# Forming the sample queries of the cross-attention in the stream of sample keys, and starting the output projection with head 3's rows

## The chip, the core and the metric

The kernel runs on one core of a Trainium2 chip. The metric is the device time of one execution in microseconds (us). TensorE (PE) multiplies matrices into PSUM; VectorE (DVE), ScalarE (ACT) and GpSimd (POOL) do the rest; SyncE (SP), ACT and POOL issue the transfers (DMA). Each engine takes its instructions in one fixed order, which was settled when the program was built, and waits at an instruction until what it needs is there.

## The reference, cut to what matters

The reference is one layer of a decoder for 1024 prompt tokens and 8 sample sequences of 4 tokens (32 tokens). The part that the change touches is the cross-attention of 4 heads of 256 channels to 256 memory tokens. The prompt attends to a memory computed in the kernel, each sample sequence to its own cached keys and values:

```python
    xn = rms_norm(x, p['ln2_g'])
    cq = rms_norm((xn @ p['ca_wq']).reshape(bsz, t, CA_HEADS, CA_HEAD_DIM), p['ca_q_norm_g'])
    s = jnp.einsum('bqhd,bmhd->bhqm', cq, mem_k.astype(cq.dtype)).astype(f32) * (CA_HEAD_DIM ** -0.5)
    pr = jax.nn.softmax(s, axis=-1).astype(x.dtype)
    co = jnp.einsum('bhqm,bmhd->bqhd', pr, mem_v.astype(x.dtype)).reshape(bsz, t, D_MODEL)
    x = x + co @ p['ca_wo']
```

## The kernel before

Every float32 product is made of three passes (`mm3`: high x high, high x low, low x high), each operand being split into a high and a low part. The 1056 columns (1024 prompt and 32 sample tokens) are worked on in three blocks, `TB`: block 0 and 1 of 384 columns, block 2 of 256 prompt and 32 sample columns.

The cross-attention runs three streams that a small planner (`par`) interleaves by weights, and a scheduler then fixes the order on each engine:

- `wq_head(h)` projects the queries of head h, blocks in the order 2, 0, 1 (PE matmuls `pp<-Xh,whi` and so on, 24 for each half head and block), and leaves the squares for their norms (`pq`), from which `query_scale` makes the scales `crs`.
- `ca_head(h)` is the prompt's attention: scores `S` (6 matmuls a tile of 128 queries), softmax on DVE and ACT, transposes of the probabilities (`pts`), products with the values (`po`). In block 2 it calls `sample_query(h)`, which scales the 32 sample queries (`pb` on PE, four products into `Qc` on DVE).
- `sample_keys(h)` waits for that, then loads the cached keys of the 8 sequences (`kt`, 256 KB each, two buffers, issued by SP), transposes each one (four PE matmuls `pt<-ident,kt`, copied to `KT` by ACT) and, after four of them, adds their scores to `Ssm`. Call these sets 1 to 8 of a head.

After head 3 comes `sample_softmax` and then the output projection `ca_wo`, with two streams: `wo_stage`, whose `part(d, b)` sums 8 row chunks of 128 (k = 0 to 7) for output chunk d and block b, and `sample_values`, which loads 16 value tiles (`vt`, 512 KB, three buffers, issued by POOL) and multiplies them (`Op`). Chunks 0 to 5 (heads 0 to 2) went to DRAM (`coT`) and are loaded again as `ms` and split to `Mh`, `Ml`; chunks 6 and 7 (head 3) stay on chip as `coh`, `col`. Block 2 of the projection waits for the end of `sample_values`.

Of the kernel before, what the change touches and what calls it, by code (L numbers as in the profile page):

```python
# [69 lines left out]
def hymba_step(ctx: ExitStack, tc: tile.TileContext, A: dict, O: dict, upto=99, dbg=None):  # L70
# [1560 lines left out]
    with ExitStack() as p5:  # L1631
# [7 lines left out]
        Qc = ca.tile([128, 2, NB, 32], F32, name="Qc", bufs=1)  # L1639
        Ssm = ps_q.tile([128, NMEM], F32, name="Ssm")  # L1640
        hq = {}
        queries = set()
        scaled, late = set(), []
        BORD = [2, 0, 1]
        CKB = 1
# [5 lines left out]
        def wq_head(h):  # L1651
            while h >= 2 and blocks[h - 2] < 3:
                yield None
            kr = ca.tile([128, 2, NMEM], F32, tag="kr", name="kr", bufs=1)
            vr = ca.tile([128, 2, 256], F32, tag="kr", name="vr", bufs=1)
            kh = ca.tile([128, 2, NMEM], F32R, tag="ckh", name="ckh")
            kl = ca.tile([128, 2, NMEM], F32R, tag="ckl", name="ckl")
            vh = ca.tile([128, 2, 256], F32R, tag="cvh", name="cvh")
            vl = ca.tile([128, 2, 256], F32R, tag="cvl", name="cvl")
            w = [load_cols(A['ca_wq'][0], 2 * h + z, GT[:, 16:24]) for z in range(2)]  # L1660
            nc.sync.dma_start(out=kr, in_=mkT_d[256 * h:256 * h + 256, :].rearrange("(k p) m -> p k m", p=128))
            split(kh, kl, kr)
            nc.sync.dma_start(out=vr, in_=mv_d[:, 256 * h:256 * h + 256].rearrange("(c p) d -> p c d", p=128))
            split(vh, vl, vr)
            cqt = {}
            ssq = ca.tile([128, 9], F32, tag="ssq", name="ssq")
            nc.vector.memset(ssq, 1.0)
            rs = ca.tile([128, 9], F32, tag="crs", name="crs")
            hq[h] = (kh, kl, vh, vl, cqt, rs)
            for oi, bi in enumerate(BORD):  # L1670
                t0, n = TB[bi]
                while h >= 1 and blocks[h - 1] < oi:
                    yield None
                ch = ca.tile([128, 2, 384], F32R, tag="ch", name="ch", bufs=4)
                cl = ca.tile([128, 2, 384], F32R, tag="cl", name="cl", bufs=4)
                sqs = []
                for z in range(2):
                    pp = ps_j.tile([128, 384], F32, tag="pj", name="pp")
                    for k in range(KD):
                        mm3(pp[:, :n], w[z][0][:, k], w[z][1][:, k], Xh[:, k, t0:t0 + n], Xl[:, k, t0:t0 + n],  # L1680
                            k == 0, k == KD - 1)
                        if k % 2:
                            yield 6 * n / 2.4
                    if late:
                        late.pop()()
                        yield 350
                    split_g(ch[:, z, :n], cl[:, z, :n], pp[:, :n], GT[:, 124 + z:125 + z])
                    sq = ca.tile([128, 384], F32, tag="csq", name="csq")
                    nc.scalar.activation(out=sq[:, :n], in_=pp[:, :n], func=AF.Square)
                    sqs.append(sq)  # L1690
                tt(out=sqs[0][:, :n], in0=sqs[0][:, :n], in1=sqs[1][:, :n], op=ALU.add)

                cqt[bi] = (ch, cl)
                late.append(lambda bi=bi, t0=t0, sq=sqs[0]: query_scale(h, bi, t0, sq, ssq, rs))
            if h == NH - 1:
                yield 700
                late.pop()()
# [23 lines left out]
        def sample_query(h, cqt, rs):  # L1721

            ch, cl = cqt[2]
            pb = ps_t.tile([128, NS], F32, tag="tp", name="pb")
            nc.tensor.matmul(pb, lhsT=rs[:NS, 8:9].to_broadcast([NS, 128]), rhs=ident[:NS, :NS], start=True, stop=True)
            cs_ = ca.tile([128, 2, NS], F32, tag="cs_", name="cs_")
            tt(out=cs_, in0=r32(ch[:, :, 256:288]), in1=r32(cl[:, :, 256:288]), op=ALU.add)
            nc.gpsimd.memset(Qc, 0.0)
            for z in range(2):
                for s in range(2):  # L1730
                    c = 16 * s + 4 * h
                    tt(out=Qc[:, z, 4 * s:4 * s + 4, c:c + 4],
                       in0=cs_[:, z, 16 * s:16 * s + 16].rearrange("p (b t) -> p b t", t=DS),
                       in1=pb[:, 16 * s:16 * s + 16].rearrange("p (b t) -> p b t", t=DS), op=ALU.mult)
            queries.add(h)

        def ca_head(h):
            while h not in hq:
# [28 lines left out]
            for oi, bi in enumerate(BORD):  # L1767
                t0, n = TB[bi]
                tl = [t for t in range(3 * bi, 3 * bi + 3) if t < 8]
                nq = 128 * len(tl)  # L1770
                Ph = ca.tile([128, 2, 384], F32R, tag="Ph", name="Ph", bufs=PB_)
                Pl = ca.tile([128, 2, 384], F32R, tag="Pl", name="Pl", bufs=PB_)
                for j, t in enumerate(tl):
                    if t in nxt_:
                        yield from score(nxt_[t])
                    P = Ps.pop(t)
                    pts = ps_t.tile([128, 2, 128], F32, tag="tp", name="pts")
                    for c in range(2):
                        nc.tensor.transpose(pts[:, c], P[:, 128 * c:128 * c + 128], ident)
                    split(Ph[:, :, 128 * j:128 * j + 128], Pl[:, :, 128 * j:128 * j + 128], pts)  # L1780
                    yield 220
                yield CA[1]
                if bi == 2:
                    sample_query(h, cqt, rs)
                for z in range(2):
                    po = ps_o.tile([128, 384], F32, tag="po", name="po")
                    for c in range(2):
                        mm3(po[:, :nq], vh[:, c, 128 * z:128 * z + 128], vl[:, c, 128 * z:128 * z + 128],
                            Ph[:, c, :nq], Pl[:, c, :nq], c == 0, c == 1)
                    if z == 1:  # L1790
                        blocks[h] = oi + 1
                    if h == NH - 1:
                        split(co_h[z][:, t0:t0 + nq], co_l[z][:, t0:t0 + nq], po[:, :nq])
                        yield 6 * nq / 2.4
                        continue
                    co = ca.tile([128, 384], F32, tag="co", name="co", bufs=2)
                    nc.scalar.copy(co[:, :nq], po[:, :nq])
                    d = 256 * h + 128 * z
                    nc.scalar.dma_start(out=coT[d:d + 128, t0:t0 + nq], in_=co[:, :nq])
                    yield 6 * nq / 2.4  # L1800

        def sample_keys(h):
            while h not in queries:
                yield None
            for s in range(2):
                KT = ca.tile([128, 4, 2, NMEM], F32, tag="KT", name="KT", bufs=CKB)
                for b4 in range(4):
                    kt = ca.tile([128, 2, 256], F32, tag="kt", name="kt", bufs=2)
                    nc.sync.dma_start(out=kt, in_=A['cache_mem_k'][0, 4 * s + b4, :, h, :].rearrange(
                        "(c p) d -> p c d", p=128))  # L1810
                    pt = ps_t.tile([128, 2, 2, 128], F32, tag="tp", name="pt")
                    for c in range(2):
                        for z in range(2):
                            nc.tensor.transpose(pt[:, z, c, :], kt[:, c, 128 * z:128 * z + 128], ident)
                    nc.scalar.copy(KT[:, b4].rearrange("p z m -> p (z m)"), pt.rearrange("p z c m -> p (z c m)"))
                    yield 440
                with tc.high_priority():
                    for z in range(2):
                        for b4 in QUADS:
                            nc.tensor.matmul(Ssm[32 * b4:32 * b4 + 32, :], lhsT=Qc[:, z, 4 * s + b4, :],  # L1820
                                             rhs=KT[:, b4, z, :], start=h == 0 and s == 0 and z == 0,
                                             stop=h == NH - 1 and s == 1 and z == 1, tile_position=(0, 32 * b4))
                yield 960
# [37 lines left out]
    with ExitStack() as p7:  # L1861
# [59 lines left out]
        def wo_stage():  # L1921
# [5 lines left out]
            def part(d, b):  # L1927
                t0, n = TB[b]
                pp = ps.tile([128, 384], F32, tag="pj", name="pp")
                for k in range(KD):  # L1930
                    mm3(pp[:, :n], w[d][0][:, k], w[d][1][:, k], Mh[k][:, t0:t0 + n], Ml[k][:, t0:t0 + n],
                        k == 0, k == KD - 1)
                    if k == 3:
                        yield 12 * n / 2.4
                update_x(wx, pp[:, :n], d, t0, n, d == 0)
                yield 12 * n / 2.4
# [197 lines left out]
```

## Time and profile before

| | us |
|---|---|
| Median of 3 runs (lowest, highest) | 1818.07 (1816.73, 1818.88) |
| The profiled execution, its time | 1823.91 |
| The profiled execution, its span | 1822.0 |
| Cross-attention, from about / to about | 718 / 912 |
| Output projection, from about / to about | 912 / 1040 |

Positions are us from the start of the span. Idle time of an engine is printed in brackets with what ended it. PE's clock has two levels, 2.4 GHz (granted clock 1.0) and 1.2 GHz (0.5).

### The profile page before, as it was taken

How to read it: one execution, taken by the hardware profiler on the slowest of the kernel's cores; microseconds unless marked ns; L12 is line 12 of the kernel's file. 1: busy time of each engine (PE TensorE's matmuls, PEld its weight loads, DVE VectorE, ACT ScalarE, POOL GpSimd, SP SyncE). 2: the span in 40 equal slices, each digit the busy share in tenths (PEclk: the TensorE clock that was granted, in tenths of full speed). 3: DMA queues.
4: the chain of work that ended last, by engine and by line, in shares of the span. 5: the costliest groups of instructions: out<-in, count | busy, mean ns of one | idle time of the engine just before them, and what ended most of it. 6: DMA issues, size and time to landing. Idle time of an engine off the chain costs nothing.

```text
span 1822.0 us, 28691 instructions
## 1 busy us (share of the span) xinstructions
PE 1713.6 (94%) x11121; PEld 1596.7 (88%) x11121; DVE 1088.7 (60%) x2563; ACT 602.8 (33%) x1368; POOL 509.3 (28%) x597
## 2 busy tenths in 40 slices
PE   8679999989797899999899999999999999999998
PEld 7458788767685899999769999999999999999997
DVE  6867635666587586555546654654654565555653
ACT  6535335566355343444433211210210211111112
POOL 4456675130300043000033332322312312322210
PEclk9878999989898999999989999999999999999999
DMA  6512232155785722323272111210211211202202
GB/s 174 217 49 80 89 87 91 40 178 172 213 270 163 263 59 64 102 91 94 84 239 70 39 40 31 70 43 28 58 48 35 58 37 46 59 25 58 58 13 97
DMA packets 151809, 170.02 MB, mean 93 GB/s; under 512 B 9528, under 2 KB 125396, under 8 KB 151675
## 3 DMA queue, kind: packets, MB, share of 16 engines
q1 hardware_dynamic: 129650, 114.04, 20.6%
q0 software_dynamic: 10944, 31.95, 5.8%
q10 hardware_dynamic: 11080, 22.21, 3.3%
q8 instruction: 87, 1.43, 0.3%
q14 instruction: 48, 0.39, 0.1%
HBM read 131.86 MB, written 36.30 MB: 92 GB/s over the span
## 4 chain that ended last, share of the span: by engine, by line
PE 79%; DVE 8%; ACT 4%; DMA 3%; issue 1%; SPq 1%; ACTq 0%; POOL 0%; DVEq 0%; POOLq 0%
PE pp L187 5%; PE pp L188 5%; PE pp L189 5%; PE pv L189 5%; PE pv L187 5%; PE pv L188 5%; PE pd L189 5%; PE pd L188 5%; PE pd L187 5%; PE pg L187 5%; PE pg L188 5%; PE pg L189 4%; PE pj L187 2%; PE S L694 2%; PE pj L189 2%; PE pj L188 2%
## 5 line engine op out<-in xcount | busy, mean ns | idle before, releaser
L56 DVE TENSOR_TENSOR xacc<-xacc,pd 128x384 f32<-128x384 f32 (+1 forms) x264 | 135.1, 518 | 169.9 <-PE pd L189 169.9
L56 ACT CAST whi<-raw 128x1024 fp32r<-128x1024 f32 x74 | 77.4, 1049 | 434.0 <-PE pg L188 332.1
L187 PE MATMUL pv<-Xh,whi 128*128 128x384 f32 (+1 forms) x528 | 172.0, 326 | 0.0
L189 PE MATMUL pv<-Xh,wlo 128*128 128x384 f32 (+1 forms) x528 | 171.7, 326 | 0.0
L188 PE MATMUL pv<-Xl,whi 128*128 128x384 f32 (+1 forms) x528 | 171.6, 325 | 0.0
L187 PE MATMUL pd<-ah,dhi 128*128 128x384 f32 (+1 forms) x528 | 171.2, 325 | 0.1
L187 PE MATMUL pg<-Xh,whi 128*128 128x384 f32 (+1 forms) x528 | 171.2, 324 | 0.0
L189 PE MATMUL pd<-ah,dlo 128*128 128x384 f32 (+1 forms) x528 | 170.9, 324 | 0.0
L188 PE MATMUL pd<-al,dhi 128*128 128x384 f32 (+1 forms) x528 | 170.1, 322 | 0.5 <-DVE al L56 0.5
L188 PE MATMUL pg<-Xl,whi 128*128 128x384 f32 (+1 forms) x528 | 170.6, 323 | 0.0
L189 PE MATMUL pg<-Xh,wlo 128*128 128x384 f32 (+1 forms) x528 | 170.1, 322 | 0.0
L56 DVE TENSOR_TENSOR wlo<-raw,whi 128x1024 fp32r<-128x1024 f32 x74 | 108.8, 1471 | 27.7 <-ACT whi L56 21.5
L799 POOL TENSOR_TENSOR raw<-raw,GT 128x1024 f32<-128x1024 f32 x30 | 69.3, 2311 | 158.8 <-DMA raw<-in_ffn_wg_dram 99.4
L187 PE MATMUL pp<-Mh,whi 128*128 128x384 f32 (+1 forms) x336 | 108.9, 329 | 2.5 <-ACT Mh L56 2.5
L187 PE MATMUL pj<-whi,Xh 128*128 128x384 f32 (+1 forms) x288 | 103.0, 360 | 8.0 <-DVE vt L56 7.5
L188 PE MATMUL pp<-Ml,whi 128*128 128x384 f32 (+1 forms) x336 | 109.6, 328 | 0.0
L189 PE MATMUL pp<-Mh,wlo 128*128 128x384 f32 (+1 forms) x336 | 109.5, 327 | 0.0
L188 PE MATMUL pj<-wlo,Xh 128*128 128x384 f32 (+1 forms) x288 | 100.5, 350 | 6.3 <-DVE wlo L56 6.3
L189 PE MATMUL pj<-whi,Xl 128*128 128x384 f32 (+1 forms) x288 | 100.8, 350 | 0.0
L189 PEld LDWEIGHTS pv<-Xh,wlo 128*128 128x128 f32 x528 | 100.0, 189 | 0.1
L187 PEld LDWEIGHTS pv<-Xh,whi 128*128 128x128 f32 x528 | 100.0, 189 | 0.0
L188 PEld LDWEIGHTS pd<-al,dhi 128*128 128x128 f32 x528 | 99.2, 188 | 0.8 <-DVE al L56 0.8
(788 smaller groups left out, 4508.8 us busy)
## 6 DMA issues: line engine op xcount, KB each, us to landing
raw<-in_ffn_wg_dram SPq DMA_DIRECT2D x22, 512.0 KB, 3.9
raw<-in_ffn_wv_dram SPq DMA_DIRECT2D x22, 512.0 KB, 3.9
raw<-in_ffn_wd_dram SPq DMA_DIRECT2D x22, 512.0 KB, 3.8
pg<-in_cache_k_dram SPq DMA_DIRECT2D x32, 256.0 KB, 3.3
V<-in_cache_v_dram SPq DMA_DIRECT2D x32, 256.0 KB, 4.1
kt<-in_cache_mem_k_dram SPq DMA_DIRECT2D x32, 256.0 KB, 3.0
vt<-in_cache_mem_v_dram POOLq DMA_DIRECT2D x16, 512.0 KB, 5.2
raw<-in_w_in_dram SPq DMA_DIRECT2D x48, 128.0 KB, 3.4
```

The costliest lines, as they stand in the source:

```text
L56: return f(*a, **k)
L187: nc.tensor.matmul(out, lhsT=wh, rhs=xh, start=start, stop=False)
L188: nc.tensor.matmul(out, lhsT=wh, rhs=xl, start=False, stop=False)
L189: nc.tensor.matmul(out, lhsT=wl, rhs=xh, start=False, stop=stop)
L694: nc.tensor.matmul(S[:, i, :w], lhsT=qT[pr, 128 * t:128 * t + 128], rhs=kT[pr, c0:c1], start=True, stop=True, tile_position=(64 * i, 0))
L799: nc.gpsimd.tensor_tensor(out=raw, in0=raw, in1=g.unsqueeze(2).to_broadcast([128, KD, 128]), op=ALU.mult)
```

## The change

`sample_keys(h)` now waits only until the scales of head h's block 2 are there and calls `sample_query` itself, so the key sets of a head come ahead of its block 2 attention. `wq_head` of the next head holds its second and third blocks back until those queries were formed. In the output projection, `part` takes the chunks in the order 6, 7, 0, 1, 2, 3, 4, 5.

```diff
-        queries = set()
+        queries, asked = {}, set()
...
             hq[h] = (kh, kl, vh, vl, cqt, rs)
+            queries[h] = (cqt, rs)
             for oi, bi in enumerate(BORD):
                 t0, n = TB[bi]
-                while h >= 1 and blocks[h - 1] < oi:
+                while h >= 1 and (blocks[h - 1] < oi or oi and h - 1 not in asked):
                     yield None
...
-            queries.add(h)
+            asked.add(h)
...
                 yield CA[1]
-                if bi == 2:
-                    sample_query(h, cqt, rs)
                 for z in range(2):
...
         def sample_keys(h):
-            while h not in queries:
+            while (h, 2) not in scaled:
                 yield None
+            sample_query(h, *queries.pop(h))
             for s in range(2):
...
-                for k in range(KD):
+                for i, k in enumerate((6, 7, 0, 1, 2, 3, 4, 5)):
                     mm3(pp[:, :n], w[d][0][:, k], w[d][1][:, k], Mh[k][:, t0:t0 + n], Ml[k][:, t0:t0 + n],
-                        k == 0, k == KD - 1)
-                    if k == 3:
+                        i == 0, i == KD - 1)
+                    if i == 3:
                         yield 12 * n / 2.4
```

The order of instructions moves with it. On PE, in the middle of head 1, these rows stood around the first `Ssm` before; sets 4 and 5 (`pt<-ident,kt`) have query projections ahead of and behind them:

```order
L188 MATMUL pp<-Xl,whi 128x384
L189 MATMUL pp<-Xh,wlo 128x384
L1814 MATMUL pt<-ident,kt 128x128 x4
L1779 MATMUL pts<-ident,P 128x128 x2
L1820 MATMUL Ssm<-KT,Qc 32x256 x8
L1703 MATMUL pq<-ones,csq 128x1 x3
L1779 MATMUL pts<-ident,P 128x128 x2
L1814 MATMUL pt<-ident,kt 128x128 x4
L187 MATMUL pp<-Xh,whi 128x384
```

Of the change, the same place on PE:

```order
L188 MATMUL pp<-Xl,whi 128x288
L189 MATMUL pp<-Xh,wlo 128x288
L1814 MATMUL pt<-ident,kt 128x128 x8
L1780 MATMUL pts<-ident,P 128x128 x2
L1820 MATMUL Ssm<-KT,Qc 32x256 x8
L1814 MATMUL pt<-ident,kt 128x128 x8
L1704 MATMUL pq<-ones,csq 128x1 x3
L1814 MATMUL pt<-ident,kt 128x128 x4
L1780 MATMUL pts<-ident,P 128x128 x2
L187 MATMUL pp<-Xh,whi 128x288
```

Sets 3 to 7 now stand together, with one pair of `pts`, one `Ssm` and one `pq` between them and no projection. Ahead of these rows, set 1 and set 2 are 20 matmuls apart, and 7 matmuls lie between set 2 and set 3. Head 2 has the same rows; head 0 has 13 and 11 projections between sets 3, 4 and 5; head 3, whose sets stand behind the last query projection, has no projection to put between.

On PE, at the start of the output projection (Mh_10217 is chunk 0, coh_7806 and coh_7807 are chunks 6 and 7), these rows followed the last `po` before:

```order
L187 MATMUL pp<-Mh_10217,whi 128x384
L188 MATMUL pp<-Ml_10223,whi 128x384
L189 MATMUL pp<-Mh_10217,wlo 128x384
L187 MATMUL pp<-Mh_10218,whi 128x384
L188 MATMUL pp<-Ml_10224,whi 128x384
L189 MATMUL pp<-Mh_10218,wlo 128x384
L1893 MATMUL Op<-vt,PT 32x256 x4
```

Of the change, from the end of the last `po` but for a few rows of chunk 6:

```order
L187 MATMUL pp<-coh_7807,whi 128x384 x2
L188 MATMUL pp<-col_7809,whi 128x384
L189 MATMUL pp<-coh_7807,wlo 128x384
L188 MATMUL pp<-col_7809,whi 128x384
L189 MATMUL pp<-coh_7807,wlo 128x384
L187 MATMUL pp<-Mh_10217,whi 128x384 x3
L188 MATMUL pp<-Ml_10223,whi 128x384
L189 MATMUL pp<-Mh_10217,wlo 128x384
L187 MATMUL pp<-Mh_10218,whi 128x384
```

30 matmuls of chunks 6 and 7, for five accumulators, now come first: 20 ahead of the last `po` and 10 behind it. Then each loaded chunk of block 0 serves three accumulators at a time, 9 matmuls where there were 3.

On PE, at the end of `sample_values`, the last two `Op` stood before as here, with 15 more projections behind them ahead of the transposes of the result (`pt<-ident,os`):

```order
L1893 MATMUL Op<-vt,PT 32x256 x4
L187 MATMUL pp<-Mh_10217,whi 128x384
L188 MATMUL pp<-Ml_10223,whi 128x384
L189 MATMUL pp<-Mh_10217,wlo 128x384
L187 MATMUL pp<-Mh_10218,whi 128x384
L188 MATMUL pp<-Ml_10224,whi 128x384
L189 MATMUL pp<-Mh_10218,wlo 128x384
L187 MATMUL pp<-Mh_10219,whi 128x384
L188 MATMUL pp<-Ml_10225,whi 128x384
L189 MATMUL pp<-Mh_10219,wlo 128x384
L1893 MATMUL Op<-vt,PT 32x256 x4
```

Of the change, the same place:

```order
L1893 MATMUL Op<-vt,PT 32x256 x4
L189 MATMUL pp<-Mh_10221,wlo 128x384
L187 MATMUL pp<-Mh_10222,whi 128x384
L188 MATMUL pp<-Ml_10228,whi 128x384
L1893 MATMUL Op<-vt,PT 32x256 x4
L189 MATMUL pp<-Mh_10222,wlo 128x384
L1893 MATMUL Op<-vt,PT 32x256 x12
L1907 MATMUL pt<-ident,os__10629 128x128 x2
L187 MATMUL pp<-coh_7806,whi 128x288 x4
```

The last three `Op` (x12) stand together, after the last projection of blocks 0 and 1, and nothing lies between them and the transposes.

## Rows read from the trace of the kernel before

**Rows 1.** Page, busy us of PE, share of the span, instructions.
```profile
PE 1713.6 (94%) x11121; PEld 1596.7 (88%) x11121; DVE 1088.7 (60%) x2563; ACT 602.8 (33%) x1368; POOL 509.3 (28%) x597
```
**Rows 2.** Stretches: length, busy us by PE, PEld, DVE, ACT, POOL; clock, DMA share, GB/s.
```profile
764.00:812.00 48.00, 46.31 (x326) 43.68 (x325) 24.97 (x98) 22.09 (x52) 0.52 (x1) 0.96 0.32 99
860.00:912.00 52.00, 45.12 (x306) 39.58 (x304) 28.57 (x114) 25.11 (x64) 0.52 (x1) 0.93 0.28 85
912.00:925.00 13.00, 10.35 (x44) 5.62 (x45) 4.49 (x9) 4.42 (x9) 4.55 (x6) 0.61 0.92 301
925.00:966.00 41.00, 40.64 (x280) 31.77 (x278) 19.39 (x38) 10.54 (x24) 12.47 (x15) 1.00 0.57 183
```
**Rows 3.** Timeline of PE: start, us, line, tiles, count; steady work, full clock.
```profile
861.86 1.04 PE L1814 MATMUL pt<-ident,kt 128*128 128x128 f32 x8
862.65 0.42 PE L188 MATMUL pp<-Xl,whi 128*128 128x384 f32 x1
...
871.23 1.07 PE L1820 MATMUL Ssm<-KT,Qc 128*32 128x256 f32 x16
...
882.52 0.33 PE L189 MATMUL po<-Ph,cvl 128*128 128x384 f32 x1
882.69 0.34 PE L189 MATMUL pp<-Xh,wlo 128*128 128x384 f32 x1
882.87 0.28 PE L187 MATMUL S<-ckh,ch 128*128 128x256 f32 x1
882.99 0.28 PE L188 MATMUL S<-ckl,ch 128*128 128x256 f32 x1
```
**Rows 4.** Timeline of PE at the end of head 2.
```profile
873.40 0.44 PE L187 MATMUL po<-Ph,cvh 128*128 128x384 f32 x1 [0.52 <-ACT Ph L56]
874.37 0.76 PE L1703 MATMUL pq<-ones,csq 128*128 128x1 f32 x6 [0.53 <-DVE Pl L56]
...
876.81 0.53 PE L187 MATMUL pp<-Xh,whi 128*128 128x384 f32 x1
...
878.64 0.34 PE L187 MATMUL pp<-Xh,whi 128*128 128x384 f32 x1
```
**Rows 5.** Tile kt, issue to landing; timeline of PE, head 3's key sets.
```profile
DMA to landing us min/median/max: 2.7/3.0/3.4
...
887.39 0.63 PE L1814 MATMUL pt<-ident,kt 128*128 128x128 f32 x4 [0.19 <-issue]
...
890.95 0.63 PE L1814 MATMUL pt<-ident,kt 128*128 128x128 f32 x4 [1.90 <-DMA kt<-in_cache_mem_k_dram]
...
905.76 0.66 PE L1814 MATMUL pt<-ident,kt 128*128 128x128 f32 x4 [1.33 <-DVE Pl L56]
...
907.09 1.07 PE L1820 MATMUL Ssm<-KT,Qc 128*32 128x256 f32 x16 [0.46 <-ACT KT L56]
```
**Rows 6.** Timeline of PE and ACT, head 3's scores to the first loaded chunks.
```profile
892.11 0.35 PE L187 MATMUL S<-ckh,ch 128*128 128x256 f32 x1
...
911.58 0.34 PE L189 MATMUL po<-Ph,cvl 128*128 128x384 f32 x1
912.89 0.69 PE L187 MATMUL pp<-Mh,whi 128*128 128x384 f32 x1 [0.98 <-ACT Mh L56]
...
914.31 0.51 ACT L56 CAST Mh<-ms 128x384 fp32r<-128x384 f32 x1 [1.47 <-DMA ms<-coT]
916.25 0.51 ACT L56 CAST Mh<-ms 128x384 fp32r<-128x384 f32 x1 [1.44 <-DMA ms<-coT]
```
**Rows 7.** Tile vt, issues and landing; timeline of PE, last Op to block 2.
```profile
L1884 POOL DMA_DIRECT2D vt<-in_cache_mem_v_dram x16: 748/748/808, 912.0 to 955.3; - x16
DMA to landing us min/median/max: 3.9/5.2/7.0
...
961.95 0.64 PE L1893 MATMUL Op<-vt,PT 128*32 128x256 f32 x8
966.59 0.80 PE L187 MATMUL pp<-Mh,whi 128*128 128x288 f32 x4 [0.94 <-ACT Mh L56]
```

## Prediction

> **What bounds the kernel now.** I read the page first: PE is busy 1713.6 of 1822.0 us [rows 1], so time moves where PE waits or runs at half clock, and any wait put into its one fixed order is paid in full. Then the stretches [rows 2]: in the middle of the cross-attention PE is busy 46.31 of 48.00 us; in its last stretch, 860 to 912, 45.12 of 52.00; in the first 13 us of the output projection 10.35, at a granted clock of 0.61; after that 40.64 of 41.00 at full clock. So two places have something to win, the end of head 3 and the start of the projection, and the middle has almost nothing to win and something to lose. Then the timeline of PE for what one instruction costs in steady work [rows 3]: 0.175 us for a 384 column matmul (882.52 to 882.69 to 882.87), 0.12 for a 256 column one, 0.40 for a key set (two sets from 861.86 to 862.65), 1.0 for the eight `Ssm` (16 passes at 871.23). A 288 column matmul I take as 0.135, between the two. At the end of a head PE waits 0.52 and 0.53 us for the split of the probabilities, and the matmuls behind that take 0.53 us where [rows 3] have 0.34: half clock until 878.64 [rows 4].
>
> **Part 1: the key sets.** The work is the same, so only waits count. `kt` has two buffers: set 3 can be loaded only when set 1 has been transposed. The trace has this cycle once without cover: set 1 of head 3 at 887.39, set 3 at 890.95 after waiting 1.90 us for its load [rows 5]. So two sets that are two apart stand at least 3.56 us apart on PE (the load itself is 2.7 to 3.4). From a set to the `Ssm` that needs its copy it is 1.33 us (905.76 to 907.09) [rows 5]. Elsewhere before, projections lie between the sets and nothing waits.
>
> Now head 1 of the change, from the start of set 1, by the rows of the new order. 20 matmuls (2.7 us) put set 2 at 3.1; 7 more put set 3 at 4.5, later than 3.56, no wait. Set 4 would follow at 4.9, but its load allows 3.1 + 3.56 = 6.7: **1.8 us**. `pts` brings PE to 7.3, `Ssm` may start at 6.7 + 1.33 = 8.0: **0.7**. It ends at 9.0, set 5 follows at once (4.5 + 3.56 is past), set 6 may start at 6.7 + 3.56 = 10.2 and PE is there at 9.4: **0.8**. `pq` to 11.3 (0.7); set 7 may start at 9.0 + 3.56 = 12.6: **1.3**. Then 23 projections cover set 8. Sum 4.6, and the same for head 2, whose rows are alike. By the chain of sets 1, 3, 5, 7 alone (10.7 us against 7.9 of work) it is 2.8, the lower bound. In head 0, 13 and 11 projections stand between sets 3, 4 and 5; the same walk leaves 0.3 ahead of set 6 and 0.9 ahead of set 7: 1.2. Together **10.4 us** for heads 0 to 2, where they had none. The waits at a head's end [rows 4] I leave as they are: in the new order of ACT the split of the probabilities still stands behind a weight split that waits for the head's projections.
>
> The Trainium skill speaks of such a load too: "DMA: Bandwidth & Descriptors", section "Anatomy of one DMA — SWDGE (gpsimd) path", fits a transfer as about 2 us and its bytes over 436 GB/s, which is an estimate of 2.6 us for 256 KB. The rows have 3.0 and decide; by the page the cycle would be some 3.2 instead of 3.56, and the sum of this part about 8.
>
> **Part 2: head 3 behind the last projection.** Before, from 882.87 to the score tile t2 at 892.11 (9.2 us) PE has 5.5 us of work, and from there to the last `po` at 911.58 (19.6) 13.3 of work [rows 6]. There, key sets lie between the steps of the softmax and fill its waits. In the change all 8 sets and both `Ssm` come ahead of t2. I walked both pieces with the same rows. To t2: 11.4 us of work (5 more sets, 2 `Ssm`, 11 `po` left over from head 2) and waits of 0.8 (the score bank, held by ACT behind the last weight split), 1.7, 0.7, 0.9, 1.3 and 0.6 at the sets and `Ssm`, and 0.8 at the `po` of block 2: 18.2 us. From t2 on the softmax chain of six tiles sets the end as before, now filled with 20 matmuls of chunks 6 and 7 (3.5 us) in place of five sets and two `Ssm` (4.0): 12.9 of work and 7.6 of waits. So the waits go from 3.7 + 6.3 to 6.8 + 7.6: **+4.4 us**. Between 1 (chunks 6 and 7 fill more) and 8 (a tile of the softmax comes one step later on ACT).
>
> **Part 3: the projection.** Before, from the end of the last `po` at 911.75 to block 2's first matmul at 966.59 it takes 54.8 us [rows 6, 7], for 192 matmuls of 0.175, 16 `Op` of 0.57 and some transposes, 43.0: 11.8 lost, 8 of them by 925, where one chunk lands about every 2 us (914.31, 916.25), feeds 3 matmuls, and PE runs at half clock [rows 2, 6]. In the change the loads start no earlier: their buffers lie where the last `po` still reads, and that `po` stays last. The 10 matmuls behind it cover 1.75 us of the 3.1 until chunk 0 is split, then each chunk feeds 9 matmuls (1.6 us). I find waits of 1.3 for chunk 0, 1.0 for chunk 1 (which stands ahead of the low pass of chunk 0), 0.7 in block 1, some 3.3 with the rest: 5 us won. But at the end the last three `Op` stand together with nothing behind them. The 15th value tile is issued when the 12th `Op` is done and lands 5.2 us after (3.9 to 7.0) [rows 7], and only 4 projections and two `Op` (1.9 us) lie between: 3.3 us of wait, and 0.7 for the 16th. Then come the 4.0 us from the last `Op` to block 2's first matmul (962.59 to 966.59), of which 15 projections covered all but 0.94 before [rows 7]. Counted through from the last `po`, the stretch comes to 50.8 us for 39.5 of work, 11.3 of waits where 11.8 were: **-0.5 us**. With the shortest landing -1.8; if the clock stays low at its start as it did before, +2.
>
> **Sum.** 10.4 + 4.4 - 0.5 = +14.3 us. Against the profiled execution, 1823.9 + 14.3 = 1838.2; it stood 5.8 above the median of the runs, so the median becomes 1818.07 + 14.3, about **1832 us**. A change of this kernel below 0.2% (3.6 us) can hardly be told from none.
>
> **Rivals.**
> - *Half clock, 1840.* Behind 1.05 us of waits PE runs at half clock to 878.64, some 3.5 us that cost half of that [rows 4]; the waits of part 1 are four times as long in each head. One more such stretch in each of heads 0 to 2 costs 1.7 when PE is busy in it, and two in the tail 3.4: +8.5 at most. Against it: much of that stretch would lie in waits that are counted already. [...] Chance 0.17.
> - *About no change, 1816 to 1821.* Part 1 at its lower bound (2.8 + 2.8 + 0.3 = 5.9), part 2 at 1, part 3 at -1.8 and another 3 us because the coT chunks, which here share the transfers with the values at 301 GB/s [rows 2], land sooner: +2. Chance 0.15.
> - *Faster, 1813.* Place: the key loads. If SP issues them early enough that every set finds its load landed, part 1 is 0 and part 2 loses the 5.2 us of waits at its sets and `Ssm`, -0.8; with part 3 that is -1.3. From there the values decide: if the last three `Op` do not wait either, 4.0 more are won, -5.3. Against it: set 3 has no second way to be loaded than into the buffer of set 1, and the shortest load of all is 2.7 [rows 5]. Chance 0.08.
> - *The change does nothing.* The orders of PE differ from head 0 on, so it is left out.
>
> **How the numbers follow.** The forecast has 0.60. The range reaches down into the no change case, to 1820 (it leaves out 0.08 and most of 0.15), and up to the half clock case, 1841. Slower: 0.60 + 0.17 = 0.77; within 0.2%: 0.15; faster: 0.08.
>
> **What would show it.** In the profile of the change: PE waiting for `kt` loads in all four heads, some 4 us in each of heads 1 and 2, where before there was one wait of 1.90; the stretch of one head, 48 us before, 51 to 53 for heads 1 and 2; the first score of t2 some 18 us after the last projection; clock and busy share at the start of the projection higher than 0.61 and 10.35 of 13; and a wait of several us for `vt` ahead of the last `Op`. The prediction is wrong if `kt` waits stay below 1 us a head, or if the last `Op` do not wait, so that the 5 us won at the start are kept.

## The result, and the profile of the changed kernel

The change makes the kernel slower: 1844.64 us median of 4 runs (1839.92 to 1849.14) against 1818.18 for the kernel before beside it, a ratio of 1.0134 (95% interval 1.0110 to 1.0158). That is 26.5 us where 14.3 were forecast, and above the range of 1820 to 1841. The profiled execution took 1844.48 us (span 1842.4), 20.6 more than the profiled execution of before, which stood some 5.8 above its runs.

On the page, PE's busy time grew by only 3.8 us [rows 1]; the span grew by 20.4, so most of the loss is idle time:

```profile
PE 1717.4 (93%) x11121; PEld 1598.8 (87%) x11121; DVE 1083.8 (59%) x2563; ACT 602.4 (33%) x1368; POOL 509.2 (28%) x597
```

Three stretches hold it: from the first score to the last query projection (heads), from there to the end of the last `po` (tail), and from there to block 2's first matmul (projection). Columns are as in [rows 2]. The tail is cut in two at the first score of head 3's tile t2, into a front piece and a back piece. The kernel before:

```profile
723.41:882.87 159.46, 155.68 (x1076) 147.60 (x1076) 85.18 (x324) 74.61 (x174) 5.47 (x5) 0.97 0.30 92
882.87:892.11 9.24, 6.34 (x49) 5.61 (x49) 7.20 (x31) 5.34 (x14) 0.00 (x0) 1.00 0.45 136
892.11:911.75 19.64, 16.79 (x122) 13.58 (x120) 11.38 (x46) 9.31 (x26) 0.00 (x0) 0.91 0.22 64
911.75:966.59 54.84, 51.16 (x324) 37.40 (x323) 24.47 (x50) 15.28 (x36) 17.02 (x21) 0.91 0.64 208
```

The changed kernel, the same cuts, the projection in two pieces; the last row is the half-clock part of the tail's front piece by itself:

```profile
722.82:889.50 166.68, 154.16 (x1065) 145.74 (x1065) 86.81 (x320) 71.53 (x168) 5.37 (x5) 0.97 0.28 87
889.50:912.76 23.26, 18.45 (x113) 14.18 (x112) 8.38 (x35) 10.54 (x24) 0.12 (x1) 0.71 0.35 108
912.76:935.35 22.59, 17.85 (x90) 15.76 (x89) 11.67 (x46) 6.60 (x20) 0.69 (x1) 0.85 0.20 59
935.35:960.00 24.65, 24.65 (x165) 19.54 (x165) 10.49 (x21) 7.53 (x17) 6.01 (x9) 1.00 0.70 227
960.00:986.27 26.27, 19.01 (x140) 12.61 (x139) 14.51 (x35) 8.69 (x25) 11.61 (x13) 0.88 0.58 178
...
898.00:911.50 13.50, 11.60 (x64) 8.58 (x68) 3.99 (x20) 4.96 (x12) 0.00 (x0) 0.50 0.24 74
```

Work moved between the stretches: 11 `po` (1.9 us) from the heads into the tail, 20 matmuls of chunks 6 and 7 (3.5 us) from the projection into the tail. Freed of that, the heads lost 166.68 + 1.9 - 159.46 = 9.1 us, the tail 45.85 - 5.4 - 28.88 = 11.6, and the projection won 0.4 (50.92 + 3.5 - 54.84). Length less busy time is idle: in the heads it went from 3.8 to 12.5 us, with the busy time, the moved `po` added, unchanged (156.1 for 155.7). In the tail idle time went from 5.8 to 9.6 only; the other 7.8 us are busy time of the same kinds of matmul, at a granted clock of 0.71 and 0.85 in its two pieces, where before had 1.00 and 0.91.

What PE waited for, of all 128 transposes of key sets: 13.5 us for loads in ten places, 1.90 us before [rows 5].

```profile
L1814 PE MATMUL pt<-ident,kt x128: 270/273/476, 732.6 to 908.8; 128*128 128x128 f32 x128
its engine sat idle before it (us, times) until:
  DMA kt<-in_cache_mem_k_dram: 13.5, 10
...
DMA to landing us min/median/max: 2.7/3.0/4.4
```

On PE's timeline of the changed kernel, first the middle of head 1, then the tail's front piece, then the end of the projection:

```profile
796.69 0.63 PE L1814 MATMUL pt<-ident,kt 128*128 128x128 f32 x4 [1.41 <-DMA kt<-in_cache_mem_k_dram]
798.08 1.07 PE L1820 MATMUL Ssm<-KT,Qc 128*32 128x256 f32 x16 [0.55 <-ACT KT L56]
800.64 0.63 PE L1814 MATMUL pt<-ident,kt 128*128 128x128 f32 x4 [0.90 <-DMA kt<-in_cache_mem_k_dram]
802.88 1.09 PE L1814 MATMUL pt<-ident,kt 128*128 128x128 f32 x4 [1.05 <-DMA kt<-in_cache_mem_k_dram]
...
898.35 1.09 PE L1814 MATMUL pt<-ident,kt 128*128 128x128 f32 x4 [3.07 <-DMA kt<-in_cache_mem_k_dram]
900.21 1.93 PE L1820 MATMUL Ssm<-KT,Qc 128*32 128x256 f32 x16 [0.34 <-ACT KT L56]
902.07 1.97 PE L1814 MATMUL pt<-ident,kt 128*128 128x128 f32 x8
906.31 1.09 PE L1814 MATMUL pt<-ident,kt 128*128 128x128 f32 x4 [0.96 <-DMA kt<-in_cache_mem_k_dram]
912.76 0.28 PE L187 MATMUL S<-ckh,ch 128*128 128x256 f32 x1
...
978.92 0.64 PE L1893 MATMUL Op<-vt,PT 128*32 128x256 f32 x8 [2.31 <-DMA vt<-in_cache_mem_v_dram]
981.28 1.08 PE L1893 MATMUL Op<-vt,PT 128*32 128x256 f32 x8 [1.73 <-DMA vt<-in_cache_mem_v_dram]
984.53 0.69 PE L1907 MATMUL pt<-ident,os__10629 128*128 128x128 f32 x2 [2.17 <-DVE os__10629 L56]
986.27 1.33 PE L187 MATMUL pp<-coh,whi 128*128 128x288 f32 x4 [1.05 <-ACT coh L56]
```

Read it so. In head 1 sets 4, 6 and 7 wait 1.41, 0.90 and 1.05 us for their loads and the first `Ssm` 0.55 for its copy, at the very places of the prediction's walk (1.8, 0.8, 1.3 and 0.7). In the tail the fourth set waits 3.07 us, and behind it a set takes 1.09 us where it took 0.63, the eight `Ssm` 1.93 where [rows 3] have 1.07: half clock, until shortly before the score at 912.76. At the end of the projection the last `Op` wait for values and what follows has no cover.

SP's queue in that place, each row a start, a time and what it issues:

```profile
891.48 0.37 SPq L1809 DMA_DIRECT2D kt<-in_cache_mem_k_dram  x1
891.90 0.46 SPq L797 DMA_DIRECT2D raw<-in_ca_wo_dram  x1
893.82 10.98 SPq L1809 DMA_DIRECT2D kt<-in_cache_mem_k_dram  x5
912.13 1.78 SPq L1875 DMA_DIRECT2D ms<-coT  x4
```

The load of the fourth set was issued at 893.82, when the second set had been transposed (from 893.19), behind a 512 KB weight load issued 1.9 us earlier. The last row is the first four `ms` loads of the projection, issued 23 us ahead of the end of the last `po`.

### The profile page after: what moved, and what is told of

Read it like the earlier page. It is cut to its first block, busy times and chain, and to the rows that moved or that the text cites. A ratio compares the mean times of both kernels' runs of the same rounds, so it can differ in the third digit from the quotient of the medians.

```text
span 1842.4 us, 28701 instructions
## 1 busy us (share of the span) xinstructions
PE 1717.4 (93%) x11121; PEld 1598.8 (87%) x11121; DVE 1083.8 (59%) x2563; ACT 602.4 (33%) x1368; POOL 509.2 (28%) x597
## 3 DMA queue, kind: packets, MB, share of 16 engines
q1 hardware_dynamic: 129650, 114.04, 20.6%
## 4 chain that ended last, share of the span: by engine, by line
PE 79%; DVE 7%; ACT 5%; DMA 4%; issue 1%; ACTq 0%; SPq 0%; DVEq 0%; POOL 0%; POOLq 0%
PE pp L187 5%; PE pp L188 5%; PE pp L189 5%; PE pv L189 5%; PE pv L187 5%; PE pv L188 5%; PE pd L189 5%; PE pd L188 5%; PE pd L187 5%; PE pg L187 5%; PE pg L188 4%; PE pg L189 4%; PE pj L187 2%; PE ov L733 1%; PE pj L189 1%; PE S L694 1%
## 5 line engine op out<-in xcount | busy, mean ns | idle before, releaser
L56 DVE TENSOR_TENSOR wlo<-raw,whi 128x1024 fp32r<-128x1024 f32 x74 | 110.3, 1492 | 18.2 <-ACT whi L56 17.9
L187 PEld LDWEIGHTS pd<-ah,dhi 128*128 128x128 f32 x528 | 99.0, 188 | 0.9 <-ACT ah L56 0.5
```

The lines of the kernel that those rows point to most:

```text
L56: return f(*a, **k)
L187: nc.tensor.matmul(out, lhsT=wh, rhs=xh, start=start, stop=False)
```

## Experiments

The theory: the moved sample queries are the whole loss and the new chunk order is about even; the loss comes from key sets that stand together against two key buffers, by the waits and by the half clock behind them. Rivals: the chunk order costs, by its value waits; the weight load on SP makes the tail's wait; the clock falls by the kind of work and not by the waits; bunched sets cost even with their keys there. The ratio is to the kernel before, which ran beside each of them (medians of 1818.97 to 1819.53); the interval is 95%. The ratio of two medians can differ from the one given by some 0.2% (queries_only: 1.0133 against 1.0113), so the table can't tell two kernels apart that lie 3 us from each other.

| kernel | median us | ratio | interval |
|---|---|---|---|
| rows_only | 1818.33 | 1.0001 | 0.9984 to 1.0017 |
| queries_only | 1843.11 | 1.0113 | 1.0082 to 1.0144 |
| head3_late | 1829.84 | 1.0054 | 1.0036 to 1.0072 |
| head3_early | 1828.42 | 1.0055 | 1.0035 to 1.0076 |
| kt_none | 1823.36 | 1.0024 | 1.0010 to 1.0039 |
| kt_five | 1823.82 | 1.0024 | 1.0009 to 1.0038 |
| kt_three | 1826.16 | 1.0039 | 1.0024 to 1.0053 |
| weights_pool | 1842.83 | 1.0129 | 1.0104 to 1.0154 |
| kt_five_head3_late | 1818.80 | 0.9990 | 0.9974 to 1.0006 |
| kt_five_before | 1817.68 | 0.9987 | 0.9967 to 1.0006 |
| kt_five_rows | 1811.97 | 0.9970 | 0.9956 to 0.9984 |
| kt_three_rows | 1812.08 | 0.9959 | 0.9943 to 0.9976 |

### Which part of the change, and which heads

**rows_only**: the kernel before with the last hunk of the diff alone.

> The kernel before with the new chunk order of the output projection alone; the cross-attention and its tail keep the order of before. Theory (the sample queries cost, the chunk order is about even): within 3 us of before, the start of the projection better than 10.35 busy of 13 us, and waits of some 4 us for value tiles at the last Op give it back. Rival (the chunk order is what costs, by its value waits at the end): 1825 or more.

**queries_only**: the change without that hunk.

> The changed kernel with the old chunk order 0 to 7: only the sample queries are moved. Theory: 1838 to 1846, about as slow as the whole change, with the projection back at its old loss of some 12 us. Rival (the chunk order costs): near 1822.

**head3_late**: the change, but head 3 forms its sample queries in its block 2.

```diff
                 yield CA[1]
+                if bi == 2 and h == NH - 1:
+                    sample_query(h, *queries.pop(h))
...
-            while (h, 2) not in scaled:
+            while (h, 2) not in scaled or h == NH - 1 and h not in asked:
                 yield None
-            sample_query(h, *queries.pop(h))
+            if h < NH - 1:
+                sample_query(h, *queries.pop(h))
```

> The changed kernel, but head 3's sample queries are formed in its block 2 as before; heads 0 to 2 keep the early ones. The tail behind the last projection has the order of before. Theory: the key loads of heads 0 to 2 alone, +8 us, about 1826. Rival (nearly all of the loss is in the tail): 1820 or less. Rival (granted clock, spread over the heads): 1835 or more.

**head3_early** is the reverse: `h < NH - 1` and `h == NH - 1` change places, and `wq_head` has its old condition.

> The reverse: heads 0 to 2 form the sample queries in block 2 as before, head 3 early. Theory: the tail alone, +12 us (the waits of the tail of the two traces differ by 11.6), about 1830; the last projection near 883, as before. Rival (the tail is slow only since it takes over what heads 0 to 2 left): 1822 or less.

The four add up within their intervals: the chunk order alone is 1.0001, the queries alone 1.0113, and the whole change 1.0134 (1.0110 to 1.0158). Heads 0 to 2 are 0.54% (9.8 us) and head 3 is 0.55% (10.0 us). So the loss is in the queries, half of it in each place; both rivals of the first two runs fall, and those of head3_late and head3_early as well. (head3_late is 4 us above its theory's 1826. head3_early came out as expected, but the 11.6 us that its theory calls waits are the tail's loss, of which 3.8 is idle time.) The stretches of rows_only say how the chunk order comes out even; the three are heads, tail and projection:

```profile
720.14:878.02 157.88, 154.10 (x1076) 146.04 (x1076) 84.96 (x324) 74.80 (x174) 5.49 (x5) 0.98 0.30 93
878.02:905.56 27.54, 21.55 (x169) 17.78 (x169) 18.50 (x77) 14.65 (x39) 0.00 (x0) 1.00 0.30 91
905.56:958.43 52.87, 47.09 (x323) 35.45 (x322) 27.37 (x55) 16.35 (x41) 18.54 (x22) 0.98 0.68 216
```

In the projection the busy time falls by 4.1 us (51.16 to 47.09), the clock rises from 0.91 to 0.98, and idle time grows by 2.1 (3.7 to 5.8): the last two `Op` wait 1.29 and 0.75 us for values, the transposes behind them 2.17 and block 2 1.06. What is left, some 2 us, is below what the runs can tell. Here heads and tail have the order of before and stand 2.9 us below its profiled execution, at a higher clock; so about half of the 5.8 us by which that execution stood above its runs lies there. Another 3.3 us lie ahead of the first score (720.14 against 723.41), where the two kernels are the same.

Of head3_early, heads and tail:

```profile
720.14:876.57 156.43, 152.65 (x1064) 144.45 (x1062) 84.10 (x323) 73.79 (x172) 5.48 (x5) 0.98 0.31 94
876.57:917.67 41.10, 31.75 (x189) 26.19 (x189) 18.31 (x77) 14.79 (x39) 0.00 (x0) 0.83 0.21 62
```

Heads 0 to 2 are untouched and the tail is slow all the same, with two waits of 2.30 and 1.79 us for keys.

### The loads taken away

**kt_none**: the change with two key tiles loaded once and used for all 32 sets; the keys of the other sequences are left out.

```diff
+        kts = {0: None, 1: None}
...
-                    kt = ca.tile([128, 2, 256], F32, tag="kt", name="kt", bufs=2)
-                    nc.sync.dma_start(out=kt, in_=A['cache_mem_k'][0, 4 * s + b4, :, h, :].rearrange(
-                        "(c p) d -> p c d", p=128))
+                    kt = kts[b4 % 2]
+                    if h == 0 and s == 0 and b4 < 2:
+                        kt = kts[b4] = ca.tile([128, 2, 256], F32, name=f"kt{b4}", bufs=1)
+                    if h == 0 and s == 0 and b4 < 2:
+                        nc.sync.dma_start(out=kt, in_=A['cache_mem_k'][0, 4 * s + b4, :, h, :].rearrange(
+                            "(c p) d -> p c d", p=128))
```

> The changed kernel without its key loads: only the first two key sets are loaded, and every later set transposes one of these two tiles again, so the keys of most sequences are left out of the result. The order on PE is nearly that of the changed kernel (6 projections move at one set of head 0, some scores by a few places). Theory (the waits for key loads are the loss in heads 0 to 2, and about half of it in the tail): the 13.5 us of kt waits go, PE's heads 0 to 2 are back within 2 us of before, 1830 to 1833 in all. Rival (the sets bunch, and the half clock behind the short transposes costs as much without a wait): 1838 or more. Rival (the loads are all of it): 1818 to 1822.

**kt_five**: the change with five key buffers. Three of them lie in tiles that stand unused just then: `PT`, written by the softmax of the samples, and `sqa`, written by the output projection.

```diff
-                    kt = ca.tile([128, 2, 256], F32, tag="kt", name="kt", bufs=2)
+                    i = (8 * h + 4 * s + b4) % 5
+                    if i < 3:
+                        kt = (PT.rearrange("p a b c -> p (a b c)"), sqa[:, 0:512], sqa[:, 512:1024])[i]
+                        kt = kt.rearrange("p (c d) -> p c d", c=2)
+                    else:
+                        kt = ca.tile([128, 2, 256], F32, tag="kt", name="kt", bufs=2)
```

> The changed kernel with all loads but five key buffers in place of two (three of them in tiles that stand unused until the softmax of the samples and the output projection), so that a load starts up to four sets ahead. Theory: as without loads, the kt waits below 3 us in all, 1830 to 1835. Rival (the loads then collide on SP behind the 512 KB weight loads): kt waits stay near 10 us and the time near 1842.

**kt_three** has one more buffer, in `PT`, in place of three.

> The changed kernel with three key buffers. Theory (a buffer's cycle of at least 3.56 us for two sets becomes one for three): waits for key loads fall from 13.5 to some 4 us, 1827 to 1833. Rival (it needs as many buffers as sets stand together, five): 1838 or more. Rival (three do): 1824.

kt_none, heads and the two pieces of the tail, and then kt_five, with its projection as a last row:

```profile
723.38:877.20 153.82, 150.03 (x1065) 141.50 (x1065) 87.29 (x320) 70.20 (x168) 5.37 (x5) 1.00 0.17 53
877.20:892.27 15.07, 13.58 (x113) 10.50 (x112) 7.29 (x32) 10.04 (x23) 0.00 (x0) 1.00 0.20 63
892.27:918.04 25.77, 20.38 (x88) 17.91 (x89) 12.52 (x50) 7.19 (x22) 0.81 (x1) 0.67 0.16 52
```

```profile
724.27:878.41 154.14, 150.09 (x1065) 141.55 (x1065) 87.55 (x320) 70.03 (x168) 5.66 (x5) 1.00 0.31 94
878.41:893.47 15.06, 13.57 (x113) 10.49 (x112) 7.28 (x32) 10.04 (x23) 0.52 (x1) 1.00 0.36 115
893.47:916.72 23.25, 18.03 (x88) 15.93 (x89) 12.32 (x50) 7.00 (x22) 0.81 (x1) 0.85 0.19 57
916.72:967.50 50.78, 43.68 (x303) 32.15 (x302) 25.06 (x55) 16.07 (x41) 17.51 (x21) 0.94 0.64 202
```

Both come out 21 us below the changed kernel, and alike: buffers do all that leaving the loads out does, so with five of them SP's queue and the transfers themselves are no limit. The theory had the direction but expected 1830 to 1835: it counted the 13.5 us of waits and not the clock; the rival that the loads are all of it (1818 to 1822) is nearer, but too low. The stretches have both waits and clock. In the heads 12.5 us come back (kt_five, which has some sets and projections at other places there): 8.5 idle (12.52 to 4.05) and 4.1 busy, the clock from 0.97 to 1.00. In the tail's front piece the same 113 instructions, in the same order, take 15.06 us in place of 23.26: 3.3 idle (4.81 to 1.49) and 4.9 busy, the clock from 0.71 to 1.00. So the half clock there came with the waits and not with the kind of work. In sum 11.8 us of idle time and 9.0 of busy time, against 20.8 by the medians. The back piece is no shorter (23.25 and 25.77 for 22.59), and its clock varies from kernel to kernel without a pattern that these runs show. In kt_three the two key waits left are 0.53 and 0.64 us, both in the tail, and its heads take 154.12 us. One buffer more is nearly all: the theory, with some 4 us of waits, left too much, and the rival that three do (1824) is nearest.

**weights_pool**: the change, the last four weight loads of the output projection issued by POOL. SP's queue then has head 3's key loads one behind the other; PE's order differs by one `po`.

```diff
-    def load_cols(w, d, g=None):
+    def load_cols(w, d, g=None, q=None):
...
-        nc.sync.dma_start(out=raw, in_=w[:, 128 * d:128 * d + 128].rearrange("(k p) c -> p k c", p=128))
+        (q or nc.sync).dma_start(out=raw, in_=w[:, 128 * d:128 * d + 128].rearrange("(k p) c -> p k c", p=128))
...
-                w[d + 4] = load_cols(wo, d + 4)
+                w[d + 4] = load_cols(wo, d + 4, q=nc.gpsimd)
```

> The changed kernel with the loads of the last four output projection weights (512 KB each) issued by POOL in place of SP, so that no weight load stands between head 3's key loads on SP; PE's order is the same but for the place of one po. Theory (the 3.07 us wait at head 3's fourth set comes from the weight load ahead of its key load, and the 13.65 us of half clock follow from that wait): the wait falls to 1.2 to 1.8, the front piece of the tail from 23.3 us to 18 to 20, the time to 1838 to 1841. Rival (two key buffers set the wait whatever stands on SP, and the clock falls anyway): within 2 us of the changed kernel.

The tail of weights_pool, front and back piece, and its timeline at the fourth set:

```profile
889.23:912.09 22.86, 18.33 (x113) 13.87 (x112) 8.11 (x35) 10.63 (x24) 1.21 (x2) 0.70 0.35 111
912.09:932.36 20.27, 15.26 (x90) 12.76 (x89) 11.65 (x47) 6.52 (x20) 0.47 (x1) 1.00 0.21 65
```

```profile
896.57 0.63 PE L1814 MATMUL pt<-ident,kt 128*128 128x128 f32 x4 [1.56 <-DMA kt<-in_cache_mem_k_dram]
897.97 1.94 PE L1820 MATMUL Ssm<-KT,Qc 128*32 128x256 f32 x16 [0.55 <-ACT KT L56]
900.77 1.94 PE L1814 MATMUL pt<-ident,kt 128*128 128x128 f32 x8 [0.86 <-DMA kt<-in_cache_mem_k_dram]
```

The wait falls to 1.56 us, as expected, and the rest does not follow: the clock falls at the next instruction all the same and the front piece stays at 22.86. So the weight load made one wait longer, and the theory that the half clock hangs on that one long wait falls: here the clock fell behind a wait of 1.56 us, with one of 0.55 at the fall and one of 0.86 behind it. The rival, two buffers whatever stands on SP, is borne out here. The back piece is 2.3 us shorter, at full clock this time, but the projection 3.3 longer (54.18 us), with value waits of 3.94, 1.46 and 0.91.

### What is left without load waits, and a faster version

**kt_five_head3_late** joins the edits of kt_five and head3_late.

> Five key buffers, new chunk order, early sample queries in heads 0 to 2 and late ones in head 3. Theory (without load waits the early queries of heads 0 to 2 cost little, since the projections behind them still fill PE, and the tail of head 3 is what is left of the loss): between 1812 and 1816, near the version with late queries in all heads. Rival (the bunched sets cost in the heads even with their keys there): 1819 or more.

It lands at the rival's edge, above the theory. By the medians the early queries of heads 0 to 2 cost some 7 us against kt_five_rows (below) even with their keys there, and head 3's another 5 (1823.82); by the ratios it is 3.6 and 6.2, so only the sum is sure. Early queries are a cost of their own: with five buffers 11.9 us by the medians (1823.82 less 1811.97) and 9.8 by the ratios, of 26.3 and 24.2 with two (1844.64 less 1818.33 of rows_only; 1.0134 less 1.0001). By the profiles of kt_five (above) and kt_five_rows, the moved work taken out, it is 4.3 us in the heads, 4.2 in the tail and 2.0 in the projection; no run took these apart further, so why early queries cost that much with their keys there stays open.

**kt_five_before** is the kernel before with five buffers alone, **kt_five_rows** with the new chunk order too, **kt_three_rows** the same with three buffers.

> The kernel before, old chunk order and late sample queries, with five key buffers. Theory (the chunk order is even, the buffers alone make the gain of some 6 us that they made with the new chunk order): 1811 to 1815. Rival (the gain needs the new chunk order): 1817 or more.

> Late sample queries as before, the new chunk order and five key buffers. Theory: one kt wait of 1.9 us in the tail is all there is to win, 1816 to 1819; before's order already hides the loads. Rival (the earlier loads let the sets move up and fill more of the tail): 1813 or less.

> Late sample queries, new chunk order, three key buffers. Theory (a third buffer lets the sets move up as five did): 1810 to 1815, faster than before. Rival (five are needed): 1817 or more.

kt_five_rows, heads, tail and projection, and then kt_three_rows:

```profile
721.52:873.25 151.73, 150.37 (x1076) 142.79 (x1076) 86.40 (x324) 73.57 (x174) 5.37 (x5) 1.00 0.31 97
873.25:902.00 28.75, 23.03 (x169) 19.56 (x169) 19.12 (x77) 14.87 (x38) 0.53 (x1) 0.94 0.20 60
902.00:954.26 52.26, 46.65 (x323) 35.57 (x322) 27.39 (x55) 16.46 (x41) 18.58 (x22) 0.97 0.68 218
```

```profile
720.97:872.66 151.69, 150.32 (x1076) 142.75 (x1075) 84.77 (x324) 73.58 (x174) 5.49 (x5) 1.00 0.31 97
872.66:901.74 29.08, 23.18 (x169) 18.93 (x169) 18.98 (x78) 15.04 (x38) 0.53 (x1) 0.94 0.25 77
901.74:953.97 52.23, 46.39 (x323) 35.65 (x322) 27.27 (x55) 16.18 (x41) 18.55 (x22) 0.97 0.67 218
```

Late queries, the new chunk order and one more key buffer beat both kernels: 1812.08 us, 0.9959 (0.9943 to 0.9976), as its theory had it. For kt_five_rows the rival (1813 or less) came true: the theory, that only one wait of 1.9 us was to be won, was too low, and looked in the wrong place. In kt_three_rows the tail is no shorter (29.08 against 27.54 in rows_only), and the heads, where before had no key wait at all, are 6.2 us shorter. Idle time there went from 3.8 to 1.4 and the clock from 0.98 to 1.00: the sets stand at other places in the order, and the half clock at a head's end [rows 4] is gone. In kt_five_before the heads are as short (151.73), but with the old chunk order its projection takes 56.0 us at a clock of 0.91; its time of 1817.68 misses what was expected and lies in the rival's range, but its interval reaches over that of kt_five_rows, so how much of the gain needs the new order stays open.

## Why the prediction was right in direction and fell short in size

- **What bounds the kernel.** Right in the main: PE's fixed order, so that waits in it are paid. That the middle has almost nothing to win was wrong. It lost 9.1 us here, but with the sets at other places (kt_three_rows) the heads were 6.2 us shorter than in rows_only: idle time and half clock, some 2 us a head, were there to be had.
- **Part 1, 10.4 us.** Right in mechanism, and in the sum with some luck. The walk gave 1.2, 4.6 and 4.6; the changed kernel waited 3.2, 4.1 and 3.4 us at the key sets and `Ssm` of heads 0, 1 and 2, 10.7 in all. From one `sample_query` to the next, head 1 took 51.8 us, inside the forecast of 51 to 53, and head 2 49.3, below it; before, they took 48.6 and 45.7. Head 0's wait was one of 3.18 us at its sixth set, whose load was issued at 745.00, behind a weight load issued at 744.22, and landed 4.3 us later; the walk knew two buffers and no weight loads on SP. The heads' ends, which the prediction left as they were, waited less, so the net loss was 9.1. By head3_late it was 9.8. The key loads, which SP issues, landed in 2.7 to 4.4 us, 3.0 in the median, and not in the 2.6 of the estimate beside this part.
- **Part 2, +4.4 us: the step that failed.** The term was mis-sized; it measured 11.6. At full clock its totals would have been right: it gave the front piece 18.2 us, and that piece takes 15.06 in kt_five, at full clock and without key waits, to which come the 3.3 of idle time that the loads cost, 18.4. It gave the back piece 20.5, and weights_pool, where that piece ran at full clock, took 20.27. How it split them was less right, and the errors cancelled: it had 11.4 us of work and 6.8 of waits in the front piece, 5.2 of them at the sets and `Ssm`; the same instructions are 13.57 busy us in kt_five, and the changed kernel idled 4.81, of which 4.62 at the sets and `Ssm`. (Part of this is only how the profile counts: four transposes ahead of a wait are 0.63 us busy [rows 5], where the walk took 0.40 from start to start.) What failed is that it took all the work at full clock. The front piece ran at 0.71 and lost another 4.9 busy us, the back piece at 0.85 and was 2.1 longer than forecast; these 7.0 are the difference of 11.6 and 4.4, but for 0.2. For the front piece kt_five shows the cause, the key waits; why the back piece ran at 0.85 stays open.
- **Part 3, -0.5 us.** Right in sum, by luck: the stretch was forecast at 50.8 and took 50.92, but with 39.5 us of work and 11.3 of waits where 43.66 busy and 7.3 idle us were measured. The start was better than the text had it: full clock and no wait from 935.35 to 960. "The loads start no earlier" was wrong, since the first four `ms` loads were issued at 912.13, 23 us ahead of the end of the last `po`. The end gave it back: 2.31 and 1.73 us for values (forecast 3.3 and 0.7), and 2.17 and 1.05 behind them, where [rows 7] have 0.94.
- **The sum against the median.** The prediction laid its 14.3 us on the median of before, though it had worked them out against an execution that stood 5.8 above it. Execution against execution the change cost 20.6 us, median against median 26.5. So of the 12.2 us that the forecast fell short, 7.2 are part 2, -1.3 part 1, 0.1 part 3 and 5.9 the difference of the two ways to compare. Of the 5.8 about half was half clock and idle time in stretches that the prediction took as its baseline, as rows_only shows; the rest lay ahead of the cross-attention.
- **The rival of half clock, 1840.** Right as a mechanism, and its sizes were partly off. It had one more stretch of half clock in each of heads 0 to 2, 1.7 us each, and 3.4 us in the tail. The stretches in the heads came, behind the key waits, and taking the loads away gave back 4.1 busy us there; but the one at each head's end [rows 4] went, so the clock of the heads is 0.97 in both kernels. In the tail it was some 7 us. The Trainium skill ("TensorE: Matmul & The Clock Gate", section "HAM oscillation — how this bites in real kernels") describes an array that goes back to half rate each time where the pieces of work are shorter than the waits for transfers between them. In the tail's front piece the waits were mostly shorter than the work between them, and the clock fell all the same: 0.71 with the key waits, 1.00 in the same 113 instructions without them.
- **About no change, and faster.** Both fell. Key sets did find their loads late, and the last `Op` did wait for values.

## What to carry to other kernels

A stream that is pulled forward and then stands together must be priced against the number of its load buffers, as the prediction did; and the price is a reason to look for one buffer more, which was worth 18 us here and was to be had in a tile that stood unused. When a walk along the order finds waits of a microsecond or more among short instructions, price the work behind them at half clock too, as the upper end of the range; in the tail that more than doubled the loss. And take the baseline of a stretch from more than one profiled execution, or set the clock of that execution against its runs.

## What the runs showed of the hardware that was not expected

The clock fell behind short waits: in the tail of weights_pool the longest wait ahead of the fall was 1.56 us, and the 113 instructions of the front piece then took 18.33 busy us in place of 13.57, nearly as much as with a wait of 3.07. And a fall can last: in the changed kernel the granted clock was 0.50 over 13.5 us in which PE was busy for 11.6.

But the length of a wait alone did not decide it. Before and rows_only have the same order in the tail. Before, a wait of 1.90 us at 890.95 [rows 5] was followed by half clock, and its back piece has a granted clock of 0.91. In rows_only the same set waited as long, and the clock was 1.00 over the whole tail:

```profile
886.12 0.63 PE L1814 MATMUL pt<-ident,kt 128*128 128x128 f32 x4 [1.93 <-DMA kt<-in_cache_mem_k_dram]
```

So the same order can pay for such a wait with half clock in one execution and not in another.
